# Strassen's sums kept in PSUM over several products, and GpSimd taken out of the FFNs

## The chip, the cores and the metric

The kernel runs on one core of a Trainium2 chip. The core has TensorE (PE, matrix products into PSUM, with PEld its weight loads), VectorE (DVE), ScalarE (ACT), GpSimd (POOL) and SyncE (SP, which here issues the DMA transfers). Each engine works through its own queue in order and waits on semaphores for the others. PSUM has eight banks of 128 x 512 fp32, which TensorE writes and ScalarE and VectorE read. The metric is the device time of one execution in microseconds; lower is better.

## The reference

The reference is one forward pass over 1024 tokens of width 1024, all in fp32, through two transformer blocks. Only the parts around the change are quoted.

```python
# first_block: mixing by MLA attention and an RWKV7 scan, then
h = rms_norm(x, norm_ffn_g[l])
gp = dwconv_centered(h @ w_ffn_gate[l], ffn_conv_w[l], ffn_conv_b[l])   # three taps along the tokens
x = x + (jax.nn.silu(gp) * (h @ w_ffn_up[l])) @ w_ffn_down[l]           # hidden width 2816
# second_block
proj = rmsnorm(x, norm1_g) @ w_in          # q, k, v, gate, ... of a gated linear attention and a conv
x = x + mixed                              # mixed = [o_gla, o_conv] @ w_out
h2 = rmsnorm(x, norm2_g[l])
x = x + (jax.nn.silu(h2 @ w_ffn_gate[l]) * (h2 @ w_ffn_up[l])) @ w_ffn_down[l]   # D_FF = 2816
return rmsnorm(x, norm_f_g)
```

## The kernel before

Activations lie transposed, features on the partitions and the 1024 tokens along the free axis. Each fp32 operand is split into a high half, made by a cast on ScalarE, and a low half, the rest, made by a subtraction on VectorE (`split`; both lines of it are recorded as L186 and L187). A product is then three matmuls of the halves, high by high, high by low and low by high.

The gate and up products of both FFNs, the projections of block 2 and the down products of both FFNs are computed in Strassen's form (Winograd's variant): a 2 x 2 block product, in blocks 512 wide, by seven products instead of eight. `ORDER` gives their order, (1, 2, 6, 5, 3, 7, 4). One such unit does the following.

- `seven` (L1099) loads two weight tiles `ra` and `rb` (tag r; `r<-wg` and `r<-wu` in the trace), forms the weight side of each product with VectorE additions (`factor`, L1086; L1091 to L1096), splits it, and issues 12 matmuls of 128 x 512 into a PSUM bank of its own for each product (L1133). Tags d and b have four banks each, eight in all. The activation side of the products is made once per matrix (`operands`, `operands2`).
- The sums of the seven products are made in SBUF: ScalarE copies product 1 out (L1110), and VectorE makes seven additions or subtractions of 128 x 512, each with one operand in PSUM (L1102). The results are G (a pair of column blocks of the gate) and V (of the up).
- `hidden` (L1144) calls `seven` once for each f of the 22 column steps. It multiplies G by the row scale `rb` of the norm, in the first FFN applies the three-tap convolution (ScalarE at L1156, VectorE at L1157 and L1158), takes Silu on ScalarE, has GpSimd multiply the result s by `rb` (L1160), and VectorE multiply it by V. After every second f, four differences of the pair are made on GpSimd (recorded as L1147), since they are the activation side of the down product, and all are written to DRAM (`d_m`, index 0 to 6, one for each product).
- `down` (L1184) has three groups of 4, 4 and 3 pairs of column steps. In each, four column steps j run through the seven products, 12 matmuls each (9 in the third group), at L1230. The next group's operands are loaded from `d_m` (`l<-d_m`) and split during a group's third and fourth step (`load`). The products are added straight into the residual tiles x0 and x1 (L1188): eight VectorE additions, one ScalarE copy (L1233, of product 1) and three GpSimd additions per step, where product 6 and product 7 are first summed with the copy and GpSimd adds that sum to the residual.
- `proj` in `block2` calls `seven` twelve times, with a product by `rb` on G and on V after it.
- In the last group, `each` hands finished residual tiles on: the sum of squares for the next norm and, at the end of the kernel, a transpose of each tile through PSUM (`flip`) whose blocks VectorE copies into eight output tiles (`turned`, L1503).

The order in which each engine runs its instructions is not the order of the code: a scheduler that simulates the engines places them when the program is built, within the limits of the tile pools (in tiles: r 3, w 4, l 4, t 8, k 2, x 28, v 2). The first unit on a new matrix (`first`) takes its products interleaved by operand, so that TensorE can begin before all operands are split.

## Time and profile before

| | before |
|---|---|
| median of 3 runs | 3138.88 us (3136.32 to 3141.7) |
| the profiled execution | 3131.96 us, span 3130.1 us |
| TensorE matmuls busy | 2985.8 us, 95% |
| VectorE busy | 2466.4 us, 79% |
| ScalarE busy | 1292.3 us, 41% |
| GpSimd busy | 794.8 us, 25% |

The page gives busy time by engine for the whole span; a busy TensorE may still run below its full clock, and the share of a stage can differ much from that of the whole. The views used further down cut the span into stages, group the instructions of a stage by line and shape, list what an engine waited for, and follow the chain of work that ended last from step to step. A row such as `t<-b,v` names tiles by their tag: output t, inputs b (a PSUM bank) and v. Durations of one instruction on VectorE overlap the next by some 0.08 us, so its pitch from start to start is a little shorter than its length.

### The profile page before, as it was taken

What the parts mean: (1) busy time and instruction counts of PE and PEld (TensorE: products, weight loads), DVE (VectorE), ACT (ScalarE), POOL (GpSimd) and SP (SyncE); (2) the same over time, 40 slices, a digit from 0 to 9 for tenths busy, and PEclk for the clock granted to TensorE, in tenths of its full rate; (3) what the DMA queues carried; (4) which work ended last, traced back from release to release, by engine and by line L of the source; (5) the groups of instructions that cost most, each with busy time, mean ns of one, the idle gap of its engine ahead of it and who ended that gap; (6) DMA issues with size and microseconds to landing.
All of it is one profiled execution on the core that took longest, in us unless ns stands there. A gap on an engine that the chain in (4) does not pass through costs nothing.

```text
span 3130.1 us, 43069 instructions
## 1 busy us (share of the span) xinstructions
PE 2985.8 (95%) x16080; PEld 2401.3 (77%) x16080; DVE 2466.4 (79%) x3755; ACT 1292.3 (41%) x2153; POOL 794.8 (25%) x638
## 2 busy tenths in 40 slices
PE   8999999999999989999999899899999999998997
PEld 6777677688888867878778677677778788887776
DVE  6597794577777766589999998976786888889887
ACT  4333322655656444343333443543333422234433
POOL 3332231132333213013223243300000122223331
PEclk9999999999999999999999999999999999999998
DMA  3444553532232335323323553223234233336421
GB/s 135 141 146 127 161 160 96 196 100 78 65 96 66 102 146 204 135 78 115 108 101 101 196 173 107 94 95 124 95 131 168 85 114 110 110 107 229 151 90 69
DMA packets 216193, 383.92 MB, mean 123 GB/s; under 512 B 67168, under 2 KB 113520, under 8 KB 215984
## 3 DMA queue, kind: packets, MB, share of 16 engines
...
## 4 chain that ended last, share of the span: by engine, by line
PE 64%; DVE 24%; DMA 4%; issue 4%; ACT 2%; POOL 2%; SPq 0%; DVEq 0%; ACTq 0%; POOLq 0%
PE d L1133 15%; PE d L934 7%; PE b L1133 6%; PE mm L206 5%; DVE w L187 5%; PE mmf L513 4%; PE d L1230 4%; PE mm L711 3%; DVE x L187 3%; PE b L1230 3%; PE po L742 2%; PE s L796 2%; DMA r<-wu 2%; DVE t L1102 2%; PE tp L733 2%
## 5 line engine op out<-in xcount | busy, mean ns | idle before, releaser
L1133 PE MATMUL d<-x,w 128*128 128x512 f32 x3120 | 753.9, 394 | 16.0 <-DVE w L187 9.6
L1133 PEld LDWEIGHTS d<-x,w 128*128 128x128 f32 x3120 | 586.4, 189 | 151.1 <-DVE w L187 15.3
L186 ACT CAST w<-r 128x512 fp32r<-128x512 f32 (+2 forms) x592 | 359.9, 621 | 645.9 <-PE d L1133 215.1
L187 DVE TENSOR_TENSOR w<-r,w 128x512 fp32r<-128x512 f32 (+2 forms) x592 | 519.4, 882 | 37.2 <-ACT w L186 36.6
L1133 PE MATMUL b<-x,w 128*128 128x512 f32 x1584 | 383.1, 390 | 5.7 <-ACT w L186 3.1
L1133 PEld LDWEIGHTS b<-x,w 128*128 128x128 f32 x1584 | 296.7, 188 | 70.7 <-ACT w L186 4.6
L1160 POOL TENSOR_TENSOR t<-t,k 128x1024 f32<-128x1024 f32 x44 | 118.8, 2700 | 760.0 <-ACT t L173 733.0
L1230 PE MATMUL d<-x,w 128*128 128x512 f32 x1056 | 272.8, 406 | 35.4 <-ACT w L186 23.0
L1230 PEld LDWEIGHTS d<-x,w 128*128 128x128 f32 x1056 | 204.1, 196 | 89.1 <-ACT w L186 29.9
L1188 POOL TENSOR_TENSOR t<-t,v 128x512 f32<-128x512 f32 x70 | 148.0, 2126 | 320.5 <-DVE v L1188 296.3
L1230 PE MATMUL b<-x,w 128*128 128x512 f32 x792 | 199.6, 395 | 4.6 <-DVE w L187 3.2
L934 PE MATMUL d<-x,w 128*128 128x512 f32 x864 | 198.4, 390 | 0.1
L934 PEld LDWEIGHTS d<-x,w 128*128 128x128 f32 x864 | 161.8, 188 | 35.1 <-DVE w L187 1.3
L1230 PEld LDWEIGHTS b<-x,w 128*128 128x128 f32 x792 | 149.8, 190 | 39.0 <-DVE w L187 4.5
L187 POOL TENSOR_TENSOR wlo<-wraw,whi 128x512 fp32r<-128x512 f32 (+2 forms) x58 | 98.2, 1695 | 277.3 <-ACT whi L186 253.0
L1091 DVE TENSOR_TENSOR r<-r 128x512 f32<-128x512 f32 (+1 forms) x80 | 61.6, 770 | 92.0 <-DMA r<-wu 72.7
L186 ACT CAST x<-l 128x512 fp32r<-128x512 f32 (+1 forms) x165 | 99.4, 640 | 64.9 <-DMA l<-d_m 55.7
L711 PE MATMUL mm<-kt,q 128*128 128x512 f32 x384 | 120.4, 424 | 0.2
L187 DVE TENSOR_TENSOR x<-l,x 128x512 fp32r<-128x512 f32 (+1 forms) x165 | 116.9, 742 | 1.9 <-ACT x L186 1.8
L186 ACT CAST whi<-wraw 128x512 fp32r<-128x512 f32 (+2 forms) x59 | 42.7, 727 | 180.9 <-PE mm L206 67.7
L513 PE MATMUL mmf<-xhi,whi 128*128 128x512 f32 x256 | 100.2, 422 | 12.0 <-DVE gu L516 12.0
L736 ACT CAST pt<-tp 128x512 fp32r<-128x512 f32 x128 | 73.9, 585 | 90.2 <-PE tp L733 89.4
...
## 6 DMA issues: line engine op xcount, KB each, us to landing
...
d_m<-t SPq DMA_DIRECT2D x110, 256.0 KB, 2.9
...
```

What stands on the lines that cost most here:

```text
L186: nc.scalar.copy(hi, src)
L187: (lo_eng or nc.gpsimd).tensor_tensor(out=lo, in0=src, in1=hi, op=ALU.subtract)
L206: nc.tensor.matmul(ps[:m, h * 512:(h + 1) * 512], a[:, c:c + m], b[:, h * 512:(h + 1) * 512], start=(k == 0 and n == 0), stop=(k == nk - 1 ...
L513: nc.tensor.matmul(ps[h], a[:, c], b[:, HALF[h]], start=(k == 0 and n == 0), stop=(k == 7 and n == 2))
L711: nc.tensor.matmul(ps, Q[a][:, c], K[b][:, HALF[hf]], start=(n == 0), stop=(n == 2))
L733: nc.tensor.transpose(tp[:, k * P:(k + 1) * P], pr[:, (hk * 4 + k) * P:(hk * 4 + k + 1) * P], self.ident)
L736: nc.scalar.copy(dst[0], t3)
L934: self.nc.tensor.matmul(p[h], a[:, c], b[:, HALF[h]], start=(k == order[0][0] and n == 0), stop=(k == order[-1][-1] and n == 2))
L1133: nc.tensor.matmul(ps[n], w[:, a], x[k][:, b], start=(k == 0 and i == 0), stop=(k == 3 and i == 2))
L1160: nc.gpsimd.tensor_tensor(out=s, in0=s, in1=rb, op=ALU.mult)
L1188: tt = lambda e, o, a, b, op: e.tensor_tensor(out=o, in0=a, in1=b, op=op)
L1230: nc.tensor.matmul(ps, w[:, a], X[k][q][:, b], start=(q == 0 and r == 0), stop=(q == n - 1 and r == 2))
```

## The change

The sums move into PSUM. In a unit of `seven`, products 1, 6, 7 and 4 accumulate in one bank, one after the other (`chain`), and 5 and 3 in another; 2 has the third. Between two products of a chain the bank's running sum is read: ScalarE copies it after 1, 5 and 6, and VectorE adds it to G or V after 2, 7 and 3, while the closing sums after 4 are read straight by the multiplication that needs them (`up`). So four of seven additions disappear, two copies come on ScalarE, and a unit uses three banks for seven. The signs of some operands change so that everything is added, with indices 4 and 5 of `d_m` swapped, and `ORDER` is now (1, 2, 6, 5, 7, 3, 4). The product of s and `rb` and the four differences per pair of steps go from GpSimd to VectorE. In `down` the same chains are read by ScalarE after 1, 6 and 7 (into v) and by VectorE for all seven additions into the residual; GpSimd has nothing to add. The interleaved start takes products 1, 2 and 5. One of the eight output tiles comes from tag k, and half of the turned blocks are copied by ScalarE.

```diff
 SILU = "silu_and_others"
-ORDER = (1, 2, 6, 5, 3, 7, 4)
+ORDER = (1, 2, 6, 5, 7, 3, 4)
...
             elif n == 4:
-                sub(b[:, L], a[:, L], b[:, L])
+                sub(b[:, L], b[:, L], a[:, L])
...
         return X, self.rbcast(acc)
-    def factor(self, n, A):
+    def factor(self, n, A, made):
...
         a, b, c, d = A
+        if n in (5, 6) and 5 not in made:
+            tt(out=c, in0=c, in1=d, op=ALU.add)
+            made.add(5)
         if n == 6:
-            tt(out=c, in0=c, in1=d, op=ALU.add)
             tt(out=a, in0=c, in1=a, op=sub)
-        elif n == 3:
+        if n in (3, 7) and 3 not in made:
             tt(out=b, in0=b, in1=a, op=sub)
-        elif n == 7:
+            made.add(3)
+        if n == 7:
...
         return {1: a, 2: b, 6: a, 5: c, 3: b, 7: a, 4: d}[n]
-    def seven(self, X, wa, wb, first, late="d", extra=(), step=None):
-        nc = self.nc
-        tt = lambda o, a, b, op: nc.vector.tensor_tensor(out=o, in0=a, in1=b, op=op)
+    def chain(self, banks, n, tags):
+        k = {1: 0, 6: 0, 7: 0, 4: 0, 2: 1, 5: 2, 3: 2}[n]
+        if n in (1, 2, 5):
+            banks[k] = self.bank(tags[k])
+        return banks[k], n in (1, 2, 5)
+    def seven(self, X, wa, wb, first, gate, up, tags=("d", "d", "d"), step=None):
+        nc = self.nc
+        add = lambda o, p: nc.vector.tensor_tensor(out=o, in0=p, in1=o, op=ALU.add)
...
         nc.sync.dma_start(out=rb, in_=wb)
-        A, W = (ra[:, L], ra[:, R], rb[:, L], rb[:, R]), {}
-        ps, done = {}, set()
-        G, V, v = self.u("t"), self.u("t"), self.t(self.U["v"], [P, 512], "v")
-        steps = [("p1", (1,), lambda: nc.scalar.copy(v, ps[1])),
-                 ("c11", (2, "p1"), lambda: tt(G[:, L], ps[2], v, ALU.add)),
-                 ("u2", (6, "c11"), lambda: tt(v, ps[6], v, ALU.add)),
-                 ("u4", (5, "u2"), lambda: tt(G[:, R], ps[5], v, ALU.add)),
-                 ("c12", (3, "u4"), lambda: tt(G[:, R], ps[3], G[:, R], ALU.add)),
-                 ("u3", (7, "u4"), lambda: tt(v, ps[7], v, ALU.add)),
-                 ("c22", (5, "u3"), lambda: tt(V[:, R], ps[5], v, ALU.add)),
-                 ("c21", (4, "u3"), lambda: tt(V[:, L], v, ps[4], ALU.subtract))]
-        steps += [(n, need, lambda go=go: go(G)) for n, need, go in extra]
+        A, W, made, banks = (ra[:, L], ra[:, R], rb[:, L], rb[:, R]), {}, set(), {}
+        G, V = self.u("t"), self.u("t")
...
         if first:
-            plan = [(n, ks) for ks in ((0, 1), (2,), (3,)) for n in ORDER[:4]] + plan[4:]
+            plan = [(n, ks) for ks in ((0, 1), (2,), (3,)) for n in (1, 2, 5)] + [(n, range(4)) for n in (6, 7, 3, 4)]
...
             if ks[0] == 0:
-                w = self.packed("w", self.factor(n, A), nc.vector)
+                w = self.packed("w", self.factor(n, A, made), nc.vector)
...
                     self.operands2(X, n)
-                W[n] = (w, X[n])
-                ps[n] = self.bank(late if n in (2, 5, 7) else "d")
-            w, x = W[n]
+                W[n] = (w, X[n], *self.chain(banks, n, tags))
+            w, x, ps, opens = W[n]
...
                 for i, (a, b) in enumerate(((c, L), (c, R), (d, L))):
-                    nc.tensor.matmul(ps[n], w[:, a], x[k][:, b], start=(k == 0 and i == 0), stop=(k == 3 and i == 2))
+                    nc.tensor.matmul(ps, w[:, a], x[k][:, b], start=(opens and k == 0 and i == 0), stop=(k == 3 and i == 2), skip_group_check=True)
             if ks[-1] == 3:
-                done.add(n)
-            for name, need, go in steps:
-                if name not in done and all(x in done for x in need):
-                    go()
-                    done.add(name)
+                if n == 1:
+                    nc.scalar.copy(G[:, L], ps)
+                elif n == 2:
+                    add(G[:, L], ps)
+                elif n == 6:
+                    nc.scalar.copy(G[:, R], ps)
+                elif n == 5:
+                    nc.scalar.copy(V[:, R], ps)
+                elif n == 7:
+                    add(V[:, R], ps)
+                elif n == 3:
+                    add(G[:, R], ps)
+                    gate(G)
+                else:
+                    up(V, ps)
...
                 self.act(SILU, s, s, AF.Silu)
-                nc.gpsimd.tensor_tensor(out=s, in0=s, in1=rb, op=ALU.mult)
+                tt(nc.vector, s, s, rb, ALU.mult)
                 got.append(s)
-            G, V = self.seven(X, wg[f], wu[f], f == 0, "b", [("act", ("c11", "c12"), act)])
+            def up(V, ps):
+                s = got[0]
+                tt(nc.vector, s[:, R], V[:, R], s[:, R], ALU.mult)
+                tt(nc.vector, s[:, L], ps, s[:, L], ALU.mult)
+            self.seven(X, wg[f], wu[f], f == 0, act, up, ("d", "b", "b"))
             s = got[0]
-            tt(nc.vector, s, V, s, ALU.mult)
...
                 out(1, s[:, L])
-                out(4, s[:, R])
+                out(5, s[:, R])
                 c = self.u("k")
-                tt(nc.gpsimd, c[:, L], s[:, R], m0[:, R], ALU.subtract)
-                out(5, c[:, L])
-                tt(nc.gpsimd, m0[:, R], m0[:, R], m0[:, L], ALU.subtract)
+                tt(nc.vector, c[:, L], s[:, R], m0[:, R], ALU.subtract)
+                out(4, c[:, L])
+                tt(nc.vector, m0[:, R], m0[:, R], m0[:, L], ALU.subtract)
                 out(3, m0[:, R])
-                tt(nc.gpsimd, c[:, R], s[:, R], m0[:, R], ALU.subtract)
+                tt(nc.vector, c[:, R], s[:, R], m0[:, R], ALU.subtract)
                 out(2, c[:, R])
-                tt(nc.gpsimd, m0[:, L], c[:, R], s[:, L], ALU.subtract)
+                tt(nc.vector, m0[:, L], s[:, L], c[:, R], ALU.subtract)
...
     def down(self, src, wd, each):
...
             nxt.update(load(0, i))
-        o = 0
+        at = 0
...
                     w = self.u("r")
-                    oq = o + q * P * 2 * e
+                    oq = at + q * P * 2 * e
...
                 x0, x1 = x[j], x[j + 4]
-                v = self.t(self.U["v"], [P, 512], "v")
+                made, banks = set(), {}
...
                     w = self.u("w", F32R)
-                    self.split(w[:, :e], w[:, e:2 * e], self.factor(k, A), nc.vector)
-                    ps = self.bank("b" if k in (2, 5, 7) else "d")
+                    self.split(w[:, :e], w[:, e:2 * e], self.factor(k, A, made), nc.vector)
+                    ps, opens = self.chain(banks, k, ("d", "b", "b"))
...
                         for r, (a, b) in enumerate(((c, L), (c, R), (d, L))):
-                            nc.tensor.matmul(ps, w[:, a], X[k][q][:, b], start=(q == 0 and r == 0), stop=(q == n - 1 and r == 2))
-                    add = lambda e, o, a: tt(e, o, o, a, ALU.add)
-                    if k == 1:
+                            nc.tensor.matmul(ps, w[:, a], X[k][q][:, b], start=(opens and q == 0 and r == 0),
+                                             stop=(q == n - 1 and r == 2), skip_group_check=True)
+                    if k in (1, 6, 7):
+                        v = self.t(self.U["v"], [P, 512], "v")
                         nc.scalar.copy(v, ps)
-                        add(nc.vector, x0[:, L], ps)
-                    elif k == 2:
-                        add(nc.vector, x0[:, L], ps)
-                    elif k == 6:
-                        add(nc.vector, v, ps)
-                        add(nc.gpsimd, x0[:, R], v)
-                    elif k == 5:
-                        add(nc.vector, x0[:, R], ps)
-                        add(nc.vector, x1[:, R], ps)
-                    elif k == 3:
-                        add(nc.vector, x0[:, R], ps)
-                        if last:
-                            each(j, x0)
-                    elif k == 7:
-                        add(nc.vector, v, ps)
-                        add(nc.vector if last and j == 3 else nc.gpsimd, x1[:, R], v)
-                        add(nc.gpsimd, x1[:, L], v)
-                    else:
-                        tt(nc.vector, x1[:, L], x1[:, L], ps, ALU.subtract)
-                        if last:
-                            each(j + 4, x1)
+                        ps = v
+                    o = {1: x0[:, L], 2: x0[:, L], 6: x0[:, R], 5: x1[:, R], 7: x1[:, R], 3: x0[:, R], 4: x1[:, L]}[k]
+                    tt(nc.vector, o, ps, o, ALU.add)
+                    if last and k in (3, 4):
+                        each(j if k == 3 else j + 4, x0 if k == 3 else x1)
...
                             nxt.update(load(gi + 1, i + 1))
-            o += KD * P * 2 * e
+            at += KD * P * 2 * e
     def block2(self, X, rb):
...
         def proj(i, j, first=False):
-            got = self.seven(X, W[i], W[j], first, extra=[("rb", ("c11", "c12"), lambda G: tt(nc.vector, G, G, rb, ALU.mult))], step=step)
-            tt(nc.vector, got[1], got[1], rb, ALU.mult)
-            return got
+            def up(V, ps):
+                tt(nc.vector, V[:, R], V[:, R], rb[:, R], ALU.mult)
+                tt(nc.vector, V[:, L], ps, rb[:, L], ALU.mult)
+            return self.seven(X, W[i], W[j], first, lambda G: tt(nc.vector, G, G, rb, ALU.mult), up, step=step)
         def kept(dst, x):
...
         nc.scalar.dma_start(out=gf, in_=I["gfin"])
-        out = [self.u("x") for _ in range(KD)]
+        out = [self.u("x") for _ in range(KD - 1)] + [self.u("k")]
...
         def turned(j, x):
...
                 for i in range(4):
-                    nc.vector.tensor_copy(out[4 * h + i][:, j * P:(j + 1) * P], ps[:, i * P:(i + 1) * P])
+                    (nc.vector.tensor_copy if h else nc.scalar.copy)(out[4 * h + i][:, j * P:(j + 1) * P], ps[:, i * P:(i + 1) * P])
         late = []

```

The change moves instructions as follows. Names carry the tile's number; a row `x3` stands for three matmuls of one weight tile. The first place is TensorE at the end of a unit of the first FFN's gate and up loop. Before, `w_2305` is the weight side of product 7, `w_2307` that of product 4, and `w_2315` and `w_2317` are those of products 1 and 2 of the next unit.

```order
4280 L1133 MATMUL b_2306_12980<-x_2240_12531,w_2305_12977 128x512 x3
4281 L1133 MATMUL d_2308_12998<-x_2243_12553,w_2307_12995 128x512 x3
4282 L1133 MATMUL d_2308_12998<-x_2244_12557,w_2307_12995 128x512 x3
4283 L1133 MATMUL d_2308_12998<-x_2245_12561,w_2307_12995 128x512 x3
4284 L1133 MATMUL d_2308_12998<-x_2246_12565,w_2307_12995 128x512 x3
4285 L1133 MATMUL d_2316_13034<-x_2149_11938,w_2315_13031 128x512 x3
4286 L1133 MATMUL d_2316_13034<-x_2169_12084,w_2315_13031 128x512 x3
4287 L1133 MATMUL d_2316_13034<-x_2189_12230,w_2315_13031 128x512 x3
4288 L1133 MATMUL d_2316_13034<-x_2209_12376,w_2315_13031 128x512 x3
4289 L1133 MATMUL b_2318_13051<-x_2150_11941,w_2317_13048 128x512 x3
```

In the changed kernel, at the same place, bank `d_2279` is the chain of 1, 6, 7 and 4 of the unit that ends, `w_2288` the weight side of its product 4, `w_2286` that of its product 3, and `d_2295` the chain of the next unit with `w_2294` for its product 1.

```order
4274 L1134 MATMUL b_2284_12917<-x_2236_12520,w_2286_12949 128x512 x3
4275 L1134 MATMUL d_2295_13009<-x_2149_11938,w_2294_13006 128x512 x3
4276 L1134 MATMUL d_2295_13009<-x_2169_12084,w_2294_13006 128x512 x3
4277 L1134 MATMUL d_2295_13009<-x_2189_12230,w_2294_13006 128x512 x3
4278 L1134 MATMUL d_2295_13009<-x_2209_12376,w_2294_13006 128x512 x2
4279 L1134 MATMUL d_2279_12865<-x_2239_12548,w_2288_12972 128x512 x3
4280 L1134 MATMUL d_2279_12865<-x_2240_12552,w_2288_12972 128x512 x3
4281 L1134 MATMUL d_2279_12865<-x_2241_12556,w_2288_12972 128x512 x3
4282 L1134 MATMUL d_2279_12865<-x_2242_12560,w_2288_12972 128x512 x3
4283 L1134 MATMUL d_2295_13009<-x_2209_12376,w_2294_13006 128x512
4284 L1134 MATMUL b_2297_13026<-x_2150_11941,w_2296_13023 128x512 x3
```

Product 4 has moved behind the next unit's product 1, eleven of whose twelve matmuls now stand between product 3 and product 4.

The second place is ScalarE in the first FFN's down product, at the change from one group to the next. Casts `x<-l` split the next group's operands as they arrive from `d_m`, casts `w<-r` the weight sides, and the copy takes product 1 out of its bank.

```order
1284 L186 CAST x_2824_16325<-l_2823_16323 128x512
1285 L186 CAST x_2825_16328<-l_2823_16323 128x512
1286 L186 CAST x_2827_16333<-l_2826_16331 128x512
1287 L186 CAST x_2828_16336<-l_2826_16331 128x512
1288 L1233 COPY v_2845_16418<-d_2847_16422 128x512
1289 L186 CAST w_2850_16454<-r_2843_16414 128x512
1290 L186 CAST x_2834_16379<-l_2833_16377 128x512
1291 L186 CAST w_2852_16474<-r_2844_16416 128x512
```

In the changed kernel the row L1249 is the copy after product 6 of a chain (`d_2681`), whose product 7 may start only when it is done.

```order
1318 L187 CAST w_2715_16214<-r_2678_16053 128x512
1319 L187 CAST x_2686_16095<-l_2685_16093 128x512
1320 L187 CAST x_2687_16098<-l_2685_16093 128x512
1321 L187 CAST x_2689_16103<-l_2688_16101 128x512
1322 L187 CAST x_2690_16106<-l_2688_16101 128x512
1323 L187 CAST w_2724_16250<-r_2679_16055 128x512
1324 L187 CAST x_2692_16111<-l_2691_16109 128x512
1325 L187 CAST x_2693_16114<-l_2691_16109 128x512
1326 L1249 COPY v_2698_16142<-d_2681_16060 128x512
```

In both, a copy of a bank stands behind casts that wait for transfers; three copies per column step stand there now for one, and two of them have a product of TensorE behind them.

## Rows read from the trace of the kernel before

**Rows 1.** Page, busy us (share of the span) and instructions by engine.

```profile
PE 2985.8 (95%) x16080; PEld 2401.3 (77%) x16080; DVE 2466.4 (79%) x3755; ACT 1292.3 (41%) x2153; POOL 794.8 (25%) x638
```

**Rows 2.** Stages, by the columns of the first line.

```profile
core 0: us, PE busy (x) PEld busy (x) DVE busy (x) ACT busy (x) POOL busy (x), PEclk, DMA share, GB/s
1336.00:1375.00 39.00, 35.71 (x148) 26.81 (x147) 36.73 (x54) 23.97 (x38) 2.38 (x1) 1.00 0.20 68
1375.00:1775.00 400.00, 392.15 (x1718) 321.32 (x1717) 380.94 (x455) 143.76 (x216) 120.48 (x60) 1.00 0.33 110
1775.00:2045.00 270.00, 239.86 (x982) 188.49 (x980) 248.21 (x366) 128.44 (x216) 89.25 (x40) 0.95 0.40 138
2045.00:2436.00 391.00, 383.87 (x1819) 304.28 (x1820) 282.80 (x425) 144.57 (x213) 20.38 (x20) 0.98 0.35 124
2436.00:2850.00 414.00, 410.86 (x1802) 337.17 (x1801) 346.41 (x448) 139.50 (x222) 113.14 (x61) 1.00 0.31 105
2850.00:3085.00 235.00, 217.75 (x923) 175.59 (x922) 208.88 (x318) 100.12 (x170) 73.07 (x36) 0.96 0.43 149
```

**Rows 3.** Chain of waits, an unhindered product: start us, us, what.

```profile
1889.80 2.72 PE b L1230 x12
```

**Rows 4.** Groups, first gate/up loop: count | busy us, mean ns | idle before.

```profile
L187 DVE TENSOR_TENSOR w<-r,w 128x512 fp32r<-128x512 f32 x140 | 137.8, 984 | 0.0
L1102 DVE TENSOR_TENSOR t<-b,v 128x512 f32<-128x512 f32 x60 | 41.1, 685 | 1.4 <-PE b L1133 0.7
L1092 DVE TENSOR_TENSOR r<-r,r 128x512 f32<-128x512 f32 x20 | 23.6, 1178 | 0.7
L1110 ACT COPY v<-d 128x512 f32<-128x512 f32 x20 | 11.6, 578 | 4.7 <-PE d L1133 4.7
```

**Rows 5.** Timeline, first gate/up loop: start us, us, engine, line, operation.

```profile
1376.08 0.68 DVE L1102 TENSOR_TENSOR t<-d,t 128x512 f32<-128x512 f32 x1
1376.68 0.68 DVE L187 TENSOR_TENSOR w<-r,w 128x512 fp32r<-128x512 f32 x1
...
1503.43 2.84 POOL L1160 TENSOR_TENSOR t<-t,k 128x1024 f32<-128x1024 f32 x1 [15.91 <-ACT t L173]
...
1504.52 2.30 DVE L187 TENSOR_TENSOR w<-r,w 128x512 fp32r<-128x512 f32 x1
```

**Rows 6.** Groups, second gate/up loop, 2475 to 2850.

```profile
L187 DVE TENSOR_TENSOR w<-r,w 128x512 fp32r<-128x512 f32 x137 | 135.4, 988 | 0.2
```

**Rows 7.** Chain of waits, GpSimd's pieces in both down products.

```profile
1864.42 7.57 POOL t L1188 x2
...
1936.35 5.16 POOL t L1188
...
1972.06 3.83 POOL t L1188
...
1990.32 4.22 POOL t L1188
...
2010.77 3.76 POOL t L1188
...
3024.52 5.18 POOL t L1188
...
3062.81 1.56 POOL t L1188
```

**Rows 8.** Groups, end of the kernel, 2850 to 3131.

```profile
L1503 DVE COPY x<-b 128x128 f32<-128x128 f32 x64 | 13.9, 278 | 0.0
```

**Rows 9.** Waits, whole span: engine, line, releaser: us, times, longest us.

```profile
ACT x L186 <- DMA l<-d_m: 55.7, 46, 5.0
```

**Rows 10.** TensorE's waits, 1775 to 2045.

```profile
PE d L1230 <- ACT w L186: 17.3, 8, 3.4
```

**Rows 11.** Timeline of TensorE, first down product.

```profile
2005.82 3.95 PE L1230 MATMUL d<-x,w 128*128 128x512 f32 x9 [3.11 <-ACT w L186]
```

**Rows 12.** Timeline of VectorE, end of the kernel.

```profile
3107.50 1.17 DVE L1188 TENSOR_TENSOR t<-t,v 128x512 f32<-128x512 f32 x1
```


## The prediction

> **What bounds the kernel now.** I read the busy line of the page first: the matmuls take 95% of the span and VectorE 79% [rows 1]. A change that leaves every matmul in place can therefore only win back what TensorE loses, and the next view says where that is. On every engine the two programs issue the same instructions in the same order, a memset and one DMA apart, up to the first matmul of the first FFN, at about 1336 us; so I cut the rest of the span into stages [rows 2]. The reader should set each stage's length against its matmul count times the pitch of an unhindered matmul, 2.72 us for 12, or 0.2267 us [rows 3]. Stage 1375 to 1775 (gate and up products of the first FFN): 400 against 1718 x 0.2267 = 389.5, a loss of 10.5 us, 7.9 of it idle. 1775 to 2045 (its down product and the start of block 2): 270 against 222.6, a loss of 47.4. 2045 to 2436 (block 2): all but 7.1 us busy. 2436 to 2850 (gate and up of the second FFN): 414 against 408.5, a loss of 5.5. 2850 to 3085 (its down product): 235 against 209.2, a loss of 25.8. That is 89 us in four stages; some records may be missing, which would make the true loss smaller. Nothing larger can be won there, and the two down products hold most of it.
>
> Next I asked what holds TensorE in those stages. In the first loop VectorE is 381 of 400 us busy [rows 2], and its commonest instruction, the low half of a weight split, takes 984 ns where the addition of the same size with an operand in PSUM takes 685 [rows 4]. The timeline shows why: GpSimd's 2.84 us product starts at 1503.43, the split started beside it takes 2.30 us and ends just after it [rows 5], while an undisturbed one takes 0.68. In the second loop the split takes 988 ns as well [rows 6], yet TensorE hardly waits there: that loop has no convolution on VectorE, so the same stall fits into its slack. In the down products the chain of waits of the first one contains GpSimd's additions into the residual, five pieces of 7.57, 5.16, 3.83, 4.22 and 3.76 us, 24.5 us in all; that of the second holds 5.18 and 1.56 [rows 7].
>
> **The change, part by part.** *Matmuls.* The same number, the same shapes; nothing. *GpSimd's work goes to VectorE, running sums go to PSUM.* Per gate/up unit VectorE gives up four 512-wide additions (seven become three; the product of V and s is still 1024 wide, in two halves). It takes on the 1024-wide product of s with the row scale and, as four pair differences per two units, two 512-wide subtractions. That is -4 + 2 + 2 halves: no net work. What goes is the stall: 140 x (984 - 685) = 41.9 us and 20 x (1178 - 685) = 9.9 us [rows 4], 52 us in the first loop. VectorE falls from 381 to about 329 of 400 and TensorE becomes the bound. The gain there is capped at the 10.5 us lost. I take 9 (4 to 10.5): the chain will still meet the loads of weights. In the second loop the same relief meets slack: 0 (-5 to +2).
>
> *ScalarE's copies.* Two more per gate/up unit, at 578 ns [rows 4]: 44 units x 2 x 0.578 = 51 us, and in the down products two more for each of 24 column steps, 28 us, and 32 of the turned copies, at VectorE's 278 ns [rows 8] 9 us. ScalarE is busy 144 of 400 and 128 of 270 us [rows 2], so I cost them at nothing as work; uncovered, they would be the whole 88 us. Their place in the queue is another matter (third rival).
>
> *Reads between the products of a chain.* Product 6 may not start before the copy of product 1 has left the bank, nor 7 before the copy of 6, 3 before that of 5, 4 before the addition of 7. The trace of before has no such wait. From below it costs 0, where another bank's product is in between; from above a whole read, 0.58 to 0.69 us, for each. The order on TensorE puts product 2 between 1 and 6, 5 between 6 and 7, and the next unit's first product between 7 and 4: at least 2.72 us for a read of 0.7. I take 0 in the loops. In block 2's 12 projections VectorE loses four additions for each, at 0.60 us from start to start [rows 5]: 12 x 4 x 0.60 = 29 us, off the path since TensorE idles only 7.1 us in that stage: +1 (-8 to +8). The three starts interleave three products by operand where four were, so three matmuls less per arriving operand hide the splits; the first start loses 39 - 148 x 0.2267 = 5.4 us now [rows 2]. I take 0 (-6 to +4).
>
> *Down, first FFN.* VectorE does seven additions per column step for eight, and none waits for GpSimd or is stalled by it. The five GpSimd pieces, 24.5 us, become additions of about 0.7 us: 24.5 - 5 x 0.7 = 21 off the chain. Not all of that is TensorE's time, for around the first piece (1864 to 1872) the splits also wait for the loads of d_m; in the whole trace such waits of ScalarE are 55.7 us [rows 9]. TensorE's waits for ScalarE's splits in the stage are 17.3 us [rows 10]; slower matmuls after a gap (nine take 3.95 us at 2005.82, for 2.04 by the pitch [rows 11]; stage clock 0.95) come on top and shrink with the gaps. I take 16 (5 to 28).
>
> *Down, second FFN.* GpSimd pieces 6.7 us, the same stalls, and 32 of the 64 turned copies leave VectorE; the loss is 25.8. I take 9 (3 to 16). *Tail.* The last product's addition no longer follows an addition from SBUF of 1.17 us [rows 12], and a GpSimd addition beside it: 2 (0 to 4).
>
> *The layout of d_m* (indices 4 and 5 swapped, two signs) moves the same bytes; SyncE issues the writes after VectorE's subtractions rather than GpSimd's: nothing.
>
> Sum: 9 + 0 + 1 + 0 + 16 + 9 + 2 = 37 us off the profiled 3131.96, or 3095. That execution is 6.9 us below the median of the runs, 3138.88, so I forecast 3138.88 - 37 = 3102.
>
> **Rivals.** *Only the loop and the tail gain.* The down products are held by loads of d_m and ScalarE's queue, not by GpSimd: for it, 17.3 us of waits name ScalarE's splits [rows 10] and 55.7 us of ScalarE's the loads [rows 9]; against it, 24.5 us of GpSimd on the chain. Gain 9 + 2 = 11: 3128.
>
> *More than forecast.* If GpSimd is behind nearly all the losses, the upper ends count: 10.5 + 28 + 16 + 4, with 6 from block 2 and the starts: 65 less, 3074. For it: stalls fall on the splits everywhere.
>
> *Chains hold TensorE: slower.* There are 56 units with four such reads and 24 column steps with three, 296 in all. If one in three is exposed for a read's 0.63 us, that is 99 x 0.63 = 62 us, against 37 won: 3138.88 + 25 = 3164. The point from which it decides is 37/0.63 = 59 exposed reads, one in five. For it: at the change of a group in the down products ScalarE's copies of the bank stand behind splits that wait for d_m, 5.0 us at worst [rows 9], and a product of TensorE now depends on them. Against it: the product of another bank stands between in the order, and there are only four such changes.
>
> By the summary of rules in the Trainium skill's "PSUM — Partial Sum Buffer", what is read while matmuls run should lie in a different bank from the one they write; a chain in one bank has to stop for its readers. Taken alone, with no product in between, that rule would expose all 296 reads, 186 us, and give 3288; no run shows such a read yet, and it is the limit of this rival with almost no chance of its own.
>
> *Nothing.* VectorE, with GpSimd's work, is as late as before: stalls go, but waits on ScalarE's identity and Silu take their place at the head of its queue. 3139 +- 6.
>
> **How the numbers follow.** Forecast 0.60, loop and tail only 0.17, more 0.09, slower by chains 0.09, nothing 0.05. The range from 3076 to 3130 holds the forecast, the first rival and part of the second; what is left out is the slow case, no change and the end of the second rival, about 0.2. A measurement of this kernel tells some 0.2% (6 us) from no change. Faster by more: 0.60 + 0.09 + most of 0.17 = 0.83; slower 0.09; within it 0.08.
>
> **What would show it.** In the profile after, GpSimd has nothing between 1340 and 1775; the low half of a split takes 0.68 to 0.75 us; VectorE's busy share in the first loop falls to about 82%, and its unit is 7 x 2.72 = 19.0 us long. The stage 1775 to 2045 is 255 us or less. I am wrong if TensorE shows waits for copies of d banks in the loops, if its waits for ScalarE in the down products stay at 17 us or grow, or if the loop stays at 400.

## The result, and the profile after

The changed kernel takes 3069.05 us, the median of 4 runs (3065.67 to 3074.57), beside 3139.97 us for the kernel before in 4 runs. The ratio is 0.9777, 95% interval 0.9759 to 0.9796: 2.2% or 71 us faster, nearly twice the 37 us forecast and 7 us below the lower end of the range. The profiled execution took 3066.92 us, span 3065.2 us.

The busy line of the page (compare [rows 1]; TensorE's instructions are the same in number), and the share of each engine in the chain that ended last, first in the kernel before, then in the changed one:

```profile
PE 2961.6 (97%) x16080; PEld 2393.9 (78%) x16080; DVE 2286.3 (75%) x3661; ACT 1374.9 (45%) x2345; POOL 390.3 (13%) x436
...
PE 64%; DVE 24%; DMA 4%; issue 4%; ACT 2%; POOL 2%; SPq 0%; DVEq 0%; ACTq 0%; POOLq 0%
...
PE 78%; DVE 12%; DMA 3%; ACT 3%; issue 2%; SPq 0%; POOL 0%; DVEq 0%; ACTq 0%; POOLq 0%
```

VectorE is busy 180 us less, GpSimd 405 us less, ScalarE 83 us more, and VectorE's share of the chain has halved. For the stages I cut both kernels at the same events: the first gate/up matmul, the last one, the last matmul of the down product, the first and the last of block 2's output product, and so on through the second FFN. The first fence is the kernel before (gate/up 1, down 1, gate/up 2, down 2; the number is that of the FFN), the second the changed one, in the same order, with block 2 up to its output product as the third row; the columns are those of [rows 2].

```profile
1336.00:1773.00 437.00, 425.86 (x1857) 346.70 (x1855) 415.68 (x504) 167.46 (x253) 122.85 (x61) 1.00 0.31 105
1773.00:2018.00 245.00, 222.26 (x927) 176.72 (x926) 223.28 (x327) 109.80 (x185) 87.57 (x39) 0.96 0.44 151
...
2436.00:2862.00 426.00, 422.86 (x1855) 347.10 (x1854) 358.41 (x468) 145.65 (x234) 113.14 (x61) 1.00 0.32 111
2862.00:3105.00 243.00, 225.75 (x970) 182.32 (x968) 215.75 (x346) 103.01 (x171) 77.22 (x39) 0.96 0.37 129
```

```profile
1334.00:1765.00 431.00, 426.44 (x1869) 350.83 (x1868) 369.21 (x514) 196.14 (x305) 0.00 (x0) 1.00 0.34 113
1765.00:1983.00 218.00, 210.39 (x911) 169.39 (x910) 189.91 (x310) 116.03 (x204) 0.00 (x0) 1.00 0.45 156
1983.00:2304.00 321.00, 310.57 (x1490) 242.63 (x1488) 228.42 (x359) 140.44 (x227) 19.14 (x20) 0.98 0.33 116
...
2394.00:2827.00 433.00, 425.98 (x1868) 351.23 (x1867) 325.65 (x471) 170.22 (x280) 0.00 (x0) 1.00 0.33 114
2827.00:3044.00 217.00, 213.60 (x957) 174.40 (x955) 179.86 (x308) 113.95 (x217) 0.00 (x0) 1.00 0.40 136
```

Lengths alone mislead here, since the changed program lets a few matmuls of one product run inside the stage of the next. So the table gives the measure of the forecast, a stage's length less its matmul count times 0.2267 us: the time that TensorE lost.

| lost, us | gate/up 1 | down 1 | gate/up 2 | down 2 | sum |
|---|---|---|---|---|---|
| before | 16.1 | 34.9 | 5.5 | 23.1 | 79.6 |
| changed | 7.4 | 11.5 | 9.6 | 0.1 | 28.6 |
| won | 8.7 | 23.4 | -4.1 | 23.0 | 51.0 |

The rest of the 64.9 us between the two spans: block 2 with its output product 417.8 to 410.5 us, the tail after the last down matmul 24.7 to 21.2, the first gate/up matmul 2.3 us earlier, and rounding of the cuts.

The first fence shows, for the changed kernel, the group of VectorE's splits in the first gate/up loop (compare [rows 4]) and the two groups of matmuls in the second down product. The second fence shows these two groups before; their line was L1230 and is L1245 now.

```profile
L188 DVE TENSOR_TENSOR w<-r,w 128x512 fp32r<-128x512 f32 x140 | 95.1, 685 | 6.1 <-ACT w L187 6.0
...
L1245 PE MATMUL d<-x,w 128*128 128x512 f32 x516 | 125.5, 391 | 3.4 <-DVE x L188 1.8 <-ACT w L187 0.9 <-ACT v L1249 0.5
L1245 PE MATMUL b<-x,w 128*128 128x512 f32 x393 | 95.8, 390 | 0.0
```

```profile
L1230 PE MATMUL d<-x,w 128*128 128x512 f32 x526 | 134.9, 405 | 13.4 <-DVE w L187 7.7 <-ACT w L186 5.6
L1230 PE MATMUL b<-x,w 128*128 128x512 f32 x396 | 100.4, 398 | 3.8 <-DVE w L187 2.8 <-DVE t L1188 0.7 <-ACT w L186 0.3
```

The 140 splits fell from 984 to 685 ns. In the down product TensorE's idle time went from 17.2 to 3.4 us and a matmul from 405 or 398 ns to 391 or 390; 526 x 14 + 396 x 8 ns is 10.5 us that the old kernel lost in slower matmuls, without standing idle; the granted clock of the stage, 0.96 over 243 us, gives about the same (0.04 x 243 = 10 us).

What the change added is in TensorE's waits over the whole span:

```profile
PE d L1134 <- ACT t L1137: 8.7, 3, 4.9
...
PE d L1134 <- ACT t L1143: 4.3, 1, 4.3
```

L1137 and L1143 are the copies of a bank after product 1 and after product 5. Three of the four waits are in the first unit on a new matrix: 1.2 us in the first FFN, 4.3 in block 2, 4.9 in the second FFN. The fourth, 2.6 us, is in block 2 too, but 93 us behind its start, where the copy stands behind activations in ScalarE's queue. The longest, on ScalarE and on TensorE, shows a copy behind casts of the operands:

```profile
2408.16 2.18 ACT L187 CAST x<-t 128x512 fp32r<-128x512 f32 x4
2410.24 0.58 ACT L1137 COPY t<-d 128x512 f32<-128x512 f32 x1
...
2410.87 1.55 PE L1134 MATMUL d<-x,w 128*128 128x512 f32 x3 [4.91 <-ACT t L1137]
```

Inside the gate/up loops there is none, and a unit has TensorE's length: the loads of two units lie (1465.90 - 1427.82)/2 = 19.04 us apart, 7 x 2.72.

```profile
1427.82 0.33 SPq L1117 DMA_DIRECT2D r<-wg  x1
...
1465.90 0.33 SPq L1117 DMA_DIRECT2D r<-wg  x1
```

In the down products TensorE's waits for ScalarE's splits, 17.3 us in the first one before [rows 10], are 2.8 us in both together:

```profile
PE d L1245 <- ACT w L187: 2.8, 4, 1.0
```

### The profile page after: what moved, and what is told of

Read it like the earlier page. It is cut to its first block, busy times and chain, and to the rows that moved or that the text cites. A ratio compares the mean times of both kernels' runs of the same rounds, so it can differ in the third digit from the quotient of the medians.

```text
span 3065.2 us, 42716 instructions
## 1 busy us (share of the span) xinstructions
PE 2961.6 (97%) x16080; PEld 2393.9 (78%) x16080; DVE 2286.3 (75%) x3661; ACT 1374.9 (45%) x2345; POOL 390.3 (13%) x436
## 4 chain that ended last, share of the span: by engine, by line
PE 78%; DVE 12%; DMA 3%; ACT 3%; issue 2%; SPq 0%; POOL 0%; DVEq 0%; ACTq 0%; POOLq 0%
PE d L1134 20%; PE b L1134 11%; PE d L935 7%; PE d L1245 6%; PE mm L207 5%; PE b L1245 4%; PE mmf L514 4%; PE mm L712 3%; PE s L797 2%; PE po L743 2%; PE tp L734 2%; DVE x L188 1%; DVE w L188 1%; PE c L842 1%; PE c L855 1%
## 5 line engine op out<-in xcount | busy, mean ns | idle before, releaser
L1134 PE MATMUL d<-x,w 128*128 128x512 f32 x3120 | 748.1, 393 | 14.4 <-ACT t L1137 8.7
L188 DVE TENSOR_TENSOR w<-r,w 128x512 fp32r<-128x512 f32 (+2 forms) x592 | 409.9, 699 | 68.5 <-ACT w L187 66.3
L1245 PE MATMUL d<-x,w 128*128 128x512 f32 x1056 | 258.1, 392 | 10.3 <-DVE w L188 4.2
L1245 PEld LDWEIGHTS d<-x,w 128*128 128x128 f32 x1056 | 196.3, 188 | 58.8 <-ACT w L187 7.0
L935 PE MATMUL d<-x,w 128*128 128x512 f32 x864 | 198.4, 389 | 0.1
L1245 PE MATMUL b<-x,w 128*128 128x512 f32 x792 | 194.1, 390 | 1.8 <-DVE t L1203 1.8
L1245 PEld LDWEIGHTS b<-x,w 128*128 128x128 f32 x792 | 148.0, 188 | 34.0 <-DVE t L1203 2.5
L1092 DVE TENSOR_TENSOR r<-r 128x512 f32<-128x512 f32 (+1 forms) x80 | 54.8, 685 | 112.1 <-DMA r<-wu 85.8
L1158 DVE TENSOR_TENSOR t<-t,k 128x1024 f32<-128x1024 f32 (+1 forms) x110 | 122.5, 1113 | 12.6 <-ACT t L174 12.3
```

The lines of the kernel that those rows point to most:

```text
L188: (lo_eng or nc.gpsimd).tensor_tensor(out=lo, in0=src, in1=hi, op=ALU.subtract)
L935: self.nc.tensor.matmul(p[h], a[:, c], b[:, HALF[h]], start=(k == order[0][0] and n == 0), stop=(k == order[-1][-1] and n == 2))
L1134: nc.tensor.matmul(ps, w[:, a], x[k][:, b], start=(opens and k == 0 and i == 0), stop=(k == 3 and i == 2), skip_group_check=True)
L1158: tt = lambda e, o, a, b, op: e.tensor_tensor(out=o, in0=a, in1=b, op=op)
L1245: nc.tensor.matmul(ps, w[:, a], X[k][q][:, b], start=(opens and q == 0 and r == 0), stop=(q == n - 1 and r == 2), skip_group_check=True)
```

## The experiments

Two theories stood against each other at first: that GpSimd's disappearance was the gain (its instructions stretch VectorE's, and VectorE waits for it), or that the sums in PSUM were (fewer operations on VectorE). Both halves of the change were undone or done alone, in the FFNs' loops and in the down products. Differences from the changed kernel go by the ratios to the kernel before, times 3139; the changed kernel has 0.9777. Every edit is scheduled anew, on all engines, so a part of a small difference can come from the order alone.

**e1: GpSimd back in the gate/up loops, sums in PSUM.**

```diff
-                tt(nc.vector, s, s, rb, ALU.mult)
+                tt(nc.gpsimd, s, s, rb, ALU.mult)
...
-                tt(nc.vector, c[:, L], s[:, R], m0[:, R], ALU.subtract)
+                tt(nc.gpsimd, c[:, L], s[:, R], m0[:, R], ALU.subtract)
```

(and the other three differences)

> The changed kernel with the product of s and the row scale and the four differences per pair of column steps back on GpSimd (110 + 44 instructions); sums stay in PSUM. VectorE is now four 512-wide operations per unit lighter than in the kernel before. Theory GpSimd (its instructions stretch VectorE's that have both operands in SBUF, and that was the loss): the splits in the first loop go back to 0.9 us or more and the loop loses part of its 13 us; with the lighter VectorE 3 to 8 us come back as loss, in the second loop 0; total 3069 + 5 to 12. Rival, fewer VectorE instructions were the gain: the loop keeps its 19.0 us per unit, total within 3 us of the changed kernel. Second question: the second down product gained 26 us where 9 were forecast; if late differences (GpSimd's writes to d_m at the end of the loop) held its start, this run loses 5 us or more between 2826 and 2870, otherwise nothing there.

Measured: 3102.9 us, ratio 0.987 (0.9855 to 0.9884), 29 us slower than the changed kernel. The stage of gate/up 1, its splits and its additions from PSUM, and one place where GpSimd runs beside one of each:

```profile
1336.00:1782.00 446.00, 429.84 (x1868) 349.78 (x1867) 364.38 (x449) 192.11 (x302) 105.57 (x61) 1.00 0.33 107
...
L188 DVE TENSOR_TENSOR w<-r,w 128x512 fp32r<-128x512 f32 x136 | 134.2, 1009 | 0.0
...
L1114 DVE TENSOR_TENSOR t<-b,t 128x512 f32<-128x512 f32 x40 | 27.4, 684 | 1.2 <-PE b L1134 1.2
...
1507.13 0.68 DVE L1114 TENSOR_TENSOR t<-b,t 128x512 f32<-128x512 f32 x1
1507.24 2.40 POOL L1158 TENSOR_TENSOR t<-t,k 128x1024 f32<-128x1024 f32 x1 [16.69 <-ACT t L174]
1507.73 2.46 DVE L188 TENSOR_TENSOR w<-r,w 128x512 fp32r<-128x512 f32 x1
```

The splits went back to 1009 ns, the additions with an operand in PSUM stayed at 684. Sorted one by one, the 30 splits of the stage that ran beside a GpSimd instruction took 2.18 us on the mean and the other 124 took 0.68 us, while the 20 additions from PSUM beside GpSimd took 0.685. The loss in this stage is 22.6 us for 7.4, more than in the kernel before; VectorE also waits 61 us there for loads of `r<-wu`, 31 in the changed kernel. Gate/up 2 lost nothing more (10.0 for 9.6). The theory of GpSimd holds in kind, and its size was underestimated: 15 us in one stage, and 7.5 and 6.3 more in the down products, in each of which GpSimd has only five late instructions, the last ones of the loop ahead. These are enough. They run in the first 45 us of the stage, a split beside them takes 2.86 us, and the granted clock there is 0.92 on the mean, 1.00 in the changed kernel. In these 45 us e1 loses 6.8 us more than the changed kernel in down 1 and 6.3 us more in down 2; the second question of the expectation is thereby answered with yes. Down 2, e1 and then the changed kernel, and the split:

```profile
2858.00:2903.00 45.00, 39.14 (x157) 30.86 (x156) 38.22 (x52) 19.79 (x34) 8.96 (x5) 0.92 0.72 253
...
2827.00:2872.00 45.00, 42.88 (x185) 34.12 (x184) 39.40 (x62) 21.26 (x37) 0.00 (x0) 1.00 0.67 238
...
2862.93 2.86 DVE L188 TENSOR_TENSOR w<-r,w 128x512 fp32r<-128x512 f32 x1
```

**e2: GpSimd back in the down products, sums in PSUM.**

```diff
-                    tt(nc.vector, o, ps, o, ALU.add)
+                    tt(nc.gpsimd if k in (1, 6, 7) else nc.vector, o, ps, o, ALU.add)
```

> The changed kernel with three of the seven residual additions per column step of the down products (those whose other operand is ScalarE's copy, after products 1, 6 and 7) on GpSimd. Sums stay in PSUM, VectorE has four additions per step. Theory GpSimd: the splits beside them stretch again and the additions of VectorE into the same residual tile wait for GpSimd, so most of the gain in both down products is lost: +25 to +45 us, 3094 to 3114. Rival, fewer VectorE instructions or the reads straight from chains were the gain: VectorE is even lighter, so within 6 us of 3069.

Measured: 3087.9 us, ratio 0.9825 (0.9809 to 0.9841), 15 us slower. By the stages only 8.0 of it are lost in down 1 and 2.3 in down 2; 6 us of the profiled execution are in block 2, which the edit does not touch, at a granted clock of 0.96. Neither theory's number: three additions on GpSimd cost a VectorE that has only four of them much less than they cost the VectorE of the kernel before.

**e3: the kernel before with its three GpSimd additions per column step moved to VectorE.**

```diff
-                        add(nc.gpsimd, x0[:, R], v)
+                        add(nc.vector, x0[:, R], v)
...
-                        add(nc.vector if last and j == 3 else nc.gpsimd, x1[:, R], v)
-                        add(nc.gpsimd, x1[:, L], v)
+                        add(nc.vector, x1[:, R], v)
+                        add(nc.vector, x1[:, L], v)
```

> The kernel before with nothing but the three GpSimd additions per column step of the down products moved to VectorE (eleven additions there instead of eight); sums in SBUF as before. Theory GpSimd: the stall and the wait go, the added 24 x 3 x 0.6 = 43 us of VectorE work lies mostly beside TensorE, so it wins 10 to 30 us: 3110 to 3130. Rival, the sums in PSUM were the gain: VectorE becomes the bound in the down products, 3140 or slower.

Measured: 3116.4 us, ratio 0.9915 (0.99 to 0.993), 27 us faster than the kernel before, though its profiled execution is only 13 us shorter than that of the kernel before, which lies 8.0 us below its median. The two down stages:

```profile
1776.00:2020.00 244.00, 224.27 (x924) 180.35 (x923) 224.01 (x363) 110.98 (x186) 9.10 (x5) 0.93 0.45 151
...
2861.00:3093.00 232.00, 220.58 (x976) 179.11 (x975) 216.83 (x381) 103.20 (x171) 11.17 (x5) 0.99 0.40 135
```

Down 2 lost 10.8 us for 23.1. Down 1 lost 34.6, as before, though all but five late instructions of GpSimd are gone from it: VectorE is as busy as it was (224 us, 223 before), with operations in the place of stalls, and TensorE waits for ScalarE's splits for 16.2 us, 17.3 before. In down 2 VectorE is as busy as before too (217 us, 216 before), and yet 12.3 us were won.

**e4: all turned copies on VectorE again.**

```diff
-                    (nc.vector.tensor_copy if h else nc.scalar.copy)(out[4 * h + i][:, j * P:(j + 1) * P], ps[:, i * P:(i + 1) * P])
+                    nc.vector.tensor_copy(out[4 * h + i][:, j * P:(j + 1) * P], ps[:, i * P:(i + 1) * P])
```

> The changed kernel with all 64 copies of the turned blocks on VectorE again, as before. If moving half of them to ScalarE was a main part of the 26 us in the second down product (9 us of copies by the forecast), 3069 + 4 to 9. If they lie beside TensorE: within 3 us, with 1 to 2 us at the tail, since the last eight copies stand on the path at the end.

Measured: 3078.9 us, ratio 0.9795 (0.978 to 0.9809), 6 us slower by the ratios, whose intervals overlap. In the profile down 2 and the tail differ by less than 1.5 us; block 2, whose instructions are the same, took 5 us more, at a granted clock of 0.96 for 0.98. So the turned copies are no part of the 23 us.

**e5: GpSimd out of the FFNs, sums in SBUF as in the kernel before.** e3, and in `hidden`:

```diff
-                nc.gpsimd.tensor_tensor(out=s, in0=s, in1=rb, op=ALU.mult)
+                nc.vector.tensor_tensor(out=s, in0=s, in1=rb, op=ALU.mult)
```

(and the four differences)

> The kernel before with GpSimd out of the FFNs and nothing else: the product of s and the row scale, the four differences per pair of steps and the three residual additions per column step of the down products all on VectorE, sums in SBUF as before. Theory GpSimd carries all: about the changed kernel's 3069 to 3080. Theory both are needed (VectorE must be lightened by the sums in PSUM to take the work over): VectorE per gate/up unit has 22 halves x 0.60 + convolution 2.4 = 15.6 plus waits for the loads of r<-wu, so the first loop keeps a loss of 5 to 15 us while the down products keep e3's gain: 3095 to 3115. Theory sums in PSUM carry all: no better than e3, 3116 or more.

**e6: sums in PSUM, GpSimd's work left to it** (the edits of e1 and e2 together).

> The changed kernel with all of GpSimd's FFN work back (what e1 and e2 moved, both): sums in PSUM and nothing else of the change but the turned copies and the start. If the two moves add up, e1's 29 and e2's 15 us by the ratios give 3069 + 44 = 3113, some 26 us faster than the kernel before, and that is what sums in PSUM are worth while GpSimd works. If GpSimd alone carried the gain: 3130 to 3142.

Measured, on one chip: e5 3091.8 us, ratio 0.9855 (0.9842 to 0.9869); e6 3107.5 us, ratio 0.9905 (0.9892 to 0.9919); the changed kernel once more (e8) 3066.8 us, ratio 0.9776 (0.9762 to 0.9789). Each half works alone: GpSimd out 45 us, sums in PSUM (with the turned copies and the start) 29 us, both 70. That GpSimd alone carries the gain is out, since e5 would have come to 3080 or less. The theory that VectorE could not take the work over without being lightened expected e5 at 3095 or more; 3091.8 is too near to decide, and the stages do: in gate/up 1 VectorE takes the work over and 4.5 us are lost for 16.1, in down 1 it does so and 30.1 are lost for 34.9. The stages of e5, and after them those of e6, in the usual order:

```profile
1336.00:1761.00 425.00, 422.70 (x1855) 347.14 (x1854) 404.99 (x567) 171.74 (x254) 0.00 (x0) 1.00 0.32 110
1761.00:2001.00 240.00, 222.67 (x926) 179.43 (x925) 223.81 (x367) 110.82 (x185) 0.00 (x0) 0.94 0.43 150
...
2413.00:2836.00 423.00, 420.99 (x1851) 346.64 (x1850) 366.79 (x531) 147.52 (x234) 0.00 (x0) 1.00 0.32 112
2836.00:3066.00 230.00, 221.01 (x981) 180.64 (x980) 214.06 (x385) 103.35 (x171) 0.00 (x0) 0.99 0.40 135
```

```profile
1335.00:1780.00 445.00, 429.81 (x1867) 349.57 (x1866) 365.31 (x449) 192.21 (x302) 105.94 (x61) 1.00 0.33 108
1780.00:2012.00 232.00, 216.00 (x915) 172.16 (x914) 196.47 (x271) 116.88 (x205) 71.63 (x41) 0.99 0.44 150
...
2426.00:2855.00 429.00, 424.00 (x1866) 349.75 (x1865) 296.80 (x409) 169.99 (x280) 110.41 (x61) 1.00 0.33 113
2855.00:3083.00 228.00, 218.31 (x959) 176.69 (x957) 188.51 (x266) 114.02 (x217) 65.97 (x41) 0.99 0.38 132
```

| lost, us | gate/up 1 | down 1 | gate/up 2 | down 2 |
|---|---|---|---|---|
| before | 16.1 | 34.9 | 5.5 | 23.1 |
| e5, GpSimd out | 4.5 | 30.1 | 3.4 | 7.6 |
| e6, sums in PSUM | 21.8 | 24.6 | 6.0 | 10.6 |
| changed, both | 7.4 | 11.5 | 9.6 | 0.1 |

In the gate/up stages GpSimd's absence does all of it, and the sums in PSUM lose 3 to 6 us on top of it. In the down products both work, and in down 1 each is worth more beside the other: GpSimd out wins 4.8 us with the sums in SBUF and 13.1 with the sums in PSUM (24.6 less 11.5).

**e9: four idle VectorE operations per column step in the changed down products.**

```diff
                     tt(nc.vector, o, ps, o, ALU.add)
+                    if k in (1, 6, 5, 7):
+                        tt(nc.vector, o, o, o, ALU.max)
```

> The changed kernel with four more VectorE operations per column step of the down products (after products 1, 6, 5 and 7 the residual half just added to is replaced by the maximum of itself and itself): eleven there, as many as with sums in SBUF and no GpSimd (e5). 24 x 4 x 0.6 = 58 us of VectorE work, no transfer, no copy, no bank more. Theory VectorE's load bounds the down products and the four operations saved by the sums in PSUM are what gained 21 and 12 us over e5 there: the two stages go back to about 240 and 229 us, total 3067 + 25 to 35. Rival, the gain came from the banks and the shorter chains of additions, not from the number of operations: less than 10 us.

Measured: 3097.9 us, ratio 0.9874 (0.9859 to 0.989), 30 us slower. The two down stages:

```profile
1766.00:1998.00 232.00, 216.03 (x914) 171.80 (x914) 214.73 (x355) 117.14 (x204) 0.00 (x0) 0.99 0.44 148
...
2846.00:3071.00 225.00, 217.24 (x957) 176.21 (x955) 204.08 (x354) 113.18 (x214) 0.00 (x0) 0.98 0.40 130
```

They lost 24.8 and 8.1 us, that is 13.3 and 8.0 more; without sums in PSUM (e5) it was 18.6 and 7.5 more. The number of VectorE operations explains most of what the sums in PSUM won there on top of e5; in down 1 some 5 us are left to something else. A further 4 us of the 30 are in block 2.

**e10: product 6 at once behind product 1.** TensorE's order is held in all units but the three first ones; the arithmetic is the same.

```diff
-        plan = [(n, range(4)) for n in ORDER]
+        plan = [(n, range(4)) for n in (1, 6, 2, 5, 7, 3, 4)]
...
+                    if not first and k == 0 and i == 0 and n == 1 and self.last4 is not None:
+                        self.after(m, self.last4)
+                    if not first and k == 0 and i == 0 and n == 2:
+                        self.after(m, last6)
...
```

> The changed kernel with TensorE's order in all gate/up units and projections but the three first ones changed so that product 6 follows product 1 at once (an order of 4 of the unit before, 1, 6, 2, 5, 7, 3): nothing stands between a bank's first product and the next one in it. 53 units. Theory of the forecast's third rival, a read between two products of a chain costs TensorE its length unless another bank's product stands in between: 0.2 us until ScalarE starts, 0.58 us of copy and 0.1 to 0.4 behind a cast, 0.8 to 1.2 us each: 53 x 0.8 to 1.2 = 42 to 64 us slower than the changed kernel, with waits of TensorE for ScalarE's copy named in the profile. Rival, TensorE does not have to wait for such a read, or its queue swallows it: within 6 us.

Measured: 3114.5 us, ratio 0.9927 (0.9912 to 0.9942), 47 us slower. The two gate/up stages, one such place on TensorE and on ScalarE, and the same product of two units in a row on TensorE:

```profile
1337.00:1790.00 453.00, 432.63 (x1866) 348.82 (x1865) 376.40 (x512) 197.43 (x305) 0.00 (x0) 1.00 0.32 107
...
2421.00:2878.00 457.00, 433.20 (x1867) 349.14 (x1866) 329.75 (x474) 172.04 (x283) 0.00 (x0) 1.00 0.32 110
...
1509.60 3.01 PE L1136 MATMUL d<-x,w 128*128 128x512 f32 x12 [0.67 <-ACT t L1147]
...
1508.97 0.58 ACT L1147 COPY t<-d 128x512 f32<-128x512 f32 x1 [1.11 <-PE d L1136]
...
1503.33 5.60 PE L1136 MATMUL d<-x,w 128*128 128x512 f32 x24
...
1523.33 5.60 PE L1136 MATMUL d<-x,w 128*128 128x512 f32 x24
```

The stages lost 30.0 and 33.8 us for 7.4 and 9.6, 46.8 us more. A steady unit takes 1523.33 - 1503.33 = 20.00 us for 19.04, so one read of 0.58 us costs 0.96 us, of which 0.67 is TensorE's wait; over 42 units that is 40 of the 46.8 us. Block 2, with its eleven such units, got no longer (320 us for 321 up to its output product); TensorE waited there for a copy after product 1 only three times, 2.9 us in all. The chain's wait is real, and in the loops only the order hides it.

**e7: four products interleaved at a start.** In the first unit on a matrix product 6 opens a bank of its own, product 1 is copied to SBUF and added back.

```diff
-            plan = [(n, ks) for ks in ((0, 1), (2,), (3,)) for n in (1, 2, 5)] + [(n, range(4)) for n in (6, 7, 3, 4)]
+            plan = [(n, ks) for ks in ((0, 1), (2,), (3,)) for n in (1, 2, 6, 5)] + [(n, range(4)) for n in (7, 3, 4)]
...
-                if n == 1:
+                if first and n == 1:
+                    nc.scalar.copy(v, ps)
+                elif first and n in (2, 6):
+                    nc.vector.tensor_tensor(out=G[:, L if n == 2 else R], in0=ps, in1=v, op=ALU.add)
+                elif first and n == 7:
+                    add(V[:, R], v)
+                    add(V[:, R], ps)
...
+                elif first:
+                    nc.vector.tensor_tensor(out=v, in0=ps, in1=v, op=ALU.add)
+                    up(V, v)
```

> An attempt to improve the changed kernel. Only the first unit on each new matrix (three of 56) differs: product 6 opens a bank of its own, so that products 1, 2, 6 and 5 can be interleaved by operand as in the kernel before, and product 1 is added back from SBUF afterwards (three more VectorE operations per such unit). In the changed kernel TensorE waits there for ScalarE's copies of a chain's bank: 1.2 us in the first FFN, 4.3 and 2.6 in block 2, 4.9 in the second FFN. If those waits are the cost of chains at a start, 6 to 13 us faster than the changed kernel run beside it; if the splits of the operands on ScalarE hold the start anyway, within 3 us.

> The changed kernel once more, on the same chip as the three others, as what they are compared with: 3069 within 5 us, or 0.978 of the kernel before. All theories expect the same.

Measured beside each other: e7 3057.8 us (3056.1 to 3063.9), e8 3066.8 us (3061.9 to 3069.0); ratios 0.9753 (0.9739 to 0.9766) and 0.9776. The medians are 9 us apart, as expected; the intervals of the ratios still overlap a little. In the profile gate/up 1 lost 4.6 us for 7.4 and gate/up 2 2.9 for 9.6, together 9.5 us less, in the stages of two of the three starts; block 2, with 4.3 us of waits at its start, is 2 us shorter, and the 2.6 us later in it stay. Two things changed at once here, since four products are interleaved again where three were: at the two FFN starts TensorE's waits for a copy (1.2 and 4.9 us) and its waits for the sums of the norm (2.2 and 2.1 us) gave way to waits of 1.8 us at each. It is the kernel with the lowest median here; e12's interval overlaps its own.

**e12: sums in SBUF in the gate/up units and the projections, in PSUM in the down products,** GpSimd out of all. The diff shows only the two orders.

```diff
 ORDER = (1, 2, 6, 5, 7, 3, 4)
+SEVEN = (1, 2, 6, 5, 3, 7, 4)
...
-        plan = [(n, range(4)) for n in ORDER]
+        plan = [(n, range(4)) for n in SEVEN]
...
```

> Sums in SBUF with seven banks in the gate/up units and the projections, as in the kernel before, but all on VectorE and ScalarE; the down products and the turned copies as in the changed kernel, sums in PSUM. (In the run named e11_hybrid the down products had stayed those of the kernel before, GpSimd's additions included, so it didn't test this.) By the stages of e5 (425 and 424 us for the two gate/up stages) and of the changed kernel (219 and 217 us for the down products): 3092 - 21 - 12 - 4 = 3055. Theory, sums in PSUM pay in the down products alone and cost 6 and 9 us at the starts of the gate/up stages: 3050 to 3060, faster than the changed kernel by 7 to 17. Rival, the lighter VectorE in the gate/up units pays too: 3067 or slower.

Measured: 3066.0 us, ratio 0.9764 (0.9746 to 0.9781), not clear of the changed kernel, 4 us by the ratios with intervals that overlap. The gate/up stages lost 4.6 and 3.4 us, as expected, but the down products 15.8 and 4.5 for 11.5 and 0.1, and together the four lost 28.3 us, the same as in the changed kernel (28.6). The expected 7 to 17 us were given back at the down products; no single wait stands out, as TensorE's idle time grew by 2.7 and 2.2 us there and the rest is slower matmuls. Its predecessor e11 had the old additions, three of them on GpSimd, in its down products beside operands laid out for the new ones, so it computes something else; its 3104.6 us answer nothing.

## Why the prediction was wrong, step by step

The sign was right, and so were the seat of the gain and the mechanism in the gate/up loop. The size was not, because the two terms of the down products were sized by the wrong thing. In the order of the sum:

- **Gate/up 1, 9 us: right.** 8.7 was won, 9.2 of it in the loop behind the first 39 us, and the signs came as written: splits at 685 ns, no GpSimd, a unit of 19.04 us, VectorE busy 369 of 431 us, 86% where 82% was forecast. Sorted by cause, GpSimd out is worth 11.6 (e5) and the sums in PSUM cost 2.9 of it.
- **Gate/up 2, 0 us: TensorE loses 4 us more,** inside the range given. That belongs to the next point.
- **The starts, 0 (-6 to +4): mis-sized, by 9 us the other way.** The term counted only how the splits of the operands are hidden; the reads between the products of a chain were priced in the steady unit alone, where the order covers them. At the starts the copies stand in ScalarE's queue behind the splits, and TensorE waits 10.4 us for them in three places. e7, which at the starts alone takes the long chain apart and interleaves four products again, wins 9 us by both together; the range for this term reached only to -6.
- **Down 1, 16 us, and down 2, 9 us: the steps that failed.** 23.4 and 23.0 were won, 46 for 25. (The 47.4 us that the prediction counted as lost around down 1 held the start of block 2 too; the stage itself lost 34.9.) I sized both by GpSimd's pieces in the chain of waits, 24.5 and 6.7 us [rows 7], and counted the sums in PSUM as one addition less per step. Both were wrong. The chain names only who comes last at each step, and its pieces are no price. GpSimd out alone (e3, e5) wins 0.3 and 4.8 us of the 34.9 in down 1, where its pieces were 24.5: the three operations per step that VectorE takes over fill what the stalls leave. In down 2, where its pieces were 6.7, the same edits win 12.3 and 15.5 of 23.1. The sums in PSUM win 10.3 and 12.5 alone (e6) and 18.6 and 7.5 on top of e5, since VectorE then has seven operations per step where it would have eleven; it is busy 190 and 180 us, for 223 and 216 before, and e9, which puts four operations back, loses 13.3 and 8.0 us. So down 1 needs both halves, and the gain there follows VectorE's load. In down 2 half to two thirds of the gain came with GpSimd's absence alone, with VectorE as busy as before (217 and 214 us in e3 and e5); through which waits is open, and VectorE's own waits for GpSimd's additions, 7.4 us there before, are among what went. That 23.4 lies inside the range for down 1 (5 to 28) is luck, since the pieces that the range was built on were not what was won; 23.0 lies outside that for down 2 (3 to 16).
- **The lower clock was named and not priced.** Both down stages of the kernel before have a granted clock of 0.96; it is 1.00 in the changed one. In down 2 that is about 10 of the 23 us. The forecast's measure of loss included it, but the gain was taken from GpSimd's pieces.
- **Block 2, +1 (-8 to +8): 7 won,** in the range. Not all of that is the change's: between programs with the same instructions there (the changed kernel, e4, e9) the stage varies by 4 to 5 us with the granted clock, 0.98 to 0.96.
- **Tail, 2 us:** 3.5, in the range.
- **From the profile to the median: 6 us.** The profiled execution of before was 8.0 us below the median of its four runs, that of after 2.1 below. The span fell by 64.9 us, the median by 71. The losses in the tables above are those of a fast execution of the kernel before.

With both down products at the top of their ranges the sum would have been 56, and the second rival, at 3074 with a chance of 0.09, came nearest. The range stopped at 3076, though the prediction itself had counted 25.8 us as lost in down 2, and all of that could go: 0.1 us is left.

**The rivals.** "Only the loop and the tail" is out: the down products won most. "Chains hold TensorE" did not come about, for the reason given against it, and e10 shows that it would have in the loops: 0.96 us for each exposed read, half as much again as the 0.63 that I priced. The Trainium skill's "PSUM — Partial Sum Buffer", in its summary of rules, wants a read beside running matmuls in another bank; the traces agree, in that a product which follows in the same bank waits (0.67 us in the row of e10), and one in another bank does not (no such wait in the changed kernel's gate/up loops). "Nothing" is out.

On GpSimd, the changed kernel's splits take 685 ns and those of e1 1009, while additions with an operand in PSUM take 684 in e1 too. That agrees with the Trainium skill's "SBUF — State Buffer", section "Who interferes with whom": a VectorE instruction with two SBUF inputs contends with a GpSimd instruction that reads SBUF, one with at most one such input, outside the modes that use two ports, does not.

Still open: which waits GpSimd's absence takes away in down 2 while VectorE stays as busy as before; the last 5 us of down 1 between e5 and e9; and why e12 gives back in the down products what it wins at the starts.
